# A decoder trunk on one core: residual and gate tiles turned onto feature partitions by VectorE blocks and small DMAs in place of TensorE transposes

## The chip, the cores and the metric

The kernel runs on one core of a Trainium2 chip. The metric is the device time of one execution in microseconds (us), all inputs in DRAM at the start and the output in DRAM at the end. The five engines are called PE (TensorE; its weight loads are listed apart as PEld), DVE (VectorE), ACT (ScalarE), POOL (GpSimd) and SP (SyncE, which here only issues DMAs). All tensors are fp32; for the matmuls a value is split in two parts, "hi" and "lo", in the type fp32r.

## The reference, cut to what matters

One layer on 256 tokens with 2048 features; x and every residual sum have the shape (256, 2048).

```python
h = x
h = h + hybrid_mixer(rmsnorm(h, norm_mix), w_in, ...)          # ends in a product with w_out (4096 x 2048)
h = h + memory_cross_attention(rmsnorm(h, norm_xa), mem_n, w_q, w_k, w_v, w_o)   # 4 heads of 128
h = h + swiglu(rmsnorm(h, norm_ffn), w_gate, w_up, w_down)     # 2048 -> 5632 -> 2048
return rmsnorm(h, norm_final)

def rmsnorm(x, g):
    return x * rsqrt(mean(x * x, axis=-1, keepdims=True) + 1e-5) * g
def swiglu(h, w_gate, w_up, w_down):
    return (silu(h @ w_gate) * (h @ w_up)) @ w_down
```

A product that contracts over features needs its left operand with the features on the 128 partitions. The residual tiles after `w_out` and `w_o`, and the gate tiles after `w_gate` and `w_up`, come out of PSUM with the tokens on the partitions. They have to be turned between the two products. That turning is what the change is about.

## The kernel before

**Weights.** All weights come as one stream of tiles of 128 x 1024 fp32 (512 KB), in the order in which they are used (`stream_plan`, 537 tiles). A tile is known by its kind and numbers: `("wo", n, c)` for w_out, `("q", t, c)`, `("o", n, c)`, `("g", n, c)` and `("u", n, c)` for gate and up, `("d", n, c)` for down. `load_to(k)` (lines 144 to 153) issues the loads of the stream up to tile k - 1 on SP; line 151 is the DMA, and six buffers `r` (pool "raw", bufs=6) receive them. `split_to(k)` (lines 155 to 169) makes the hi part on ACT (line 165) and the lo part on DVE (line 166), four buffers `h` and `l` each. So the load of tile i waits until the split of tile i - 6 has read its buffer, and that split waits until PE is through with tile i - 10.

**Units and steps.** The program is written as a row of units, two weight tiles each in the stages spoken of here. Of one unit:

```python
load_to(last + AHEAD - 1)        # AHEAD = 6
split_to(last + 1)
for i, (ks, fn) in enumerate(parts):
    fn()                         # the matmuls of one part
    if i == 0:
        step()                   # each waiting post-processing generator goes on to its next yield
        split_to(last + 3)
load_to(last + AHEAD)
```

What has to be done with a unit's result (evacuate, square, turn) is a generator such as `wo_post`, `o_post` or `u_post`; it is appended after the unit, and a piece of it, up to the next `yield`, is written into the program in the `step()` of each later unit. **PE and SP run strictly in the order in which the program is written** (line 112). The order on ACT, DVE and POOL is chosen when the kernel is built by a planner that works with its own assumed costs; at run time each engine follows its list in order.

**A DMA's place.** SP executes its list in order, so a DMA that waits holds all loads behind it. The DMAs of a queue engine take turns on eight completion semaphores: a DMA waits until the one eight before it has landed.

**Token-major products.** `tok_mm` (lines 789 to 798) does twelve matmuls for a weight tile: two feature blocks, two token blocks `tb`, and for each the three products of hi and lo parts (lines 796, 797, 798). The q projection contracts in the other orientation, through `mm_hi` and `mm_lo` (lines 294 and 300).

**Turning.** `add_to_res(n, ...)` (lines 808 to 814) adds the PSUM result of a column group n (512 features) to the two residual tiles (line 812) and squares them on ACT (line 814). `to_features(n, gain, dst)` (lines 816 to 827) turns the two 128 x 512 tiles with eight PE transposes of 128 x 128 into PSUM tiles `m` (line 823), and `hilo_scaled` scales and splits each of four features blocks out of PSUM: ACT line 179, DVE line 180. In `wo_post` and `o_post` it comes one step after `add_to_res`. `u_post(n)` multiplies the gate (line 1008), and one step later turns it with eight transposes (line 1015) and splits it (ACT line 1018, DVE line 1019). There are 4 groups after w_out (`"nxa"` gains), 4 after w_o (`"nffn"` gains), and 11 gate groups.

**Who needs them.** The features 8 to 15 of the first residual (groups 2 and 3) are used by `q_rest(0)`, the first q part with c = 1, which follows the four parts with c = 0. The features 2c and 2c + 1 of the second residual are used by gate tile `("g", 0, c)`, so group n is first used in c = 2n. The gate features are used only in the down stage, after all gate and up tiles.

**The order between w_o and gate.** This part is written out by hand (lines 963 to 988) and then goes on in units:

```python
ahead(("o", 1, 1), 2)     # loads up to ("g", 0, 0)
o_mm(0, 3)                # last matmuls of group 0; appends o_post(0)
step()                    # first piece of o_post(0)
o_mm(1, 3)                # last matmuls of group 1; appends o_post(1)
for n in (2, 3): unit(...)   # groups 2 and 3, two weight tiles each
```

Of the kernel before, what the change touches and what calls it, by code (L numbers as in the profile page):

```python
# [13 lines left out]
F32 = mybir.dt.float32  # L14
F32R = mybir.dt.float32r
AF = mybir.ActivationFunctionType
ALU = mybir.AluOpType
# [3 lines left out]
T = 256  # L21
# [47 lines left out]
def stream_plan():  # L69

    p = []
    p += [(("k0",), 512), (("v0",), 512)]
    for kt in range(1, KT):
        p.append((("kv", kt), 1024))
    p += [(("a", t, c), 1024) for c in range(2) for t in FIRST]
    for _, m, t, _ in mixer_order():
        p += [((m, t, c), 1024) for c in range(2)]
    for n in range(4):
        p += [(("wo", n, c), 1024) for c in range(KT)]
    p += [(("q", t, c), 1024) for c in range(2) for t in range(4)]  # L80
    p += [(("o", n, c), 1024) for n, c in [(0, 0), (1, 0), (0, 1), (1, 1), (2, 0), (2, 1), (3, 0), (3, 1)]]
    for n in range(FN):
        for m in "gu":
            p += [((m, n, c), 1024) for c in range(KT // 2)]
    for n in range(4):
        p += [(("d", n, c), 1024) for c in range(FT // 2)]
    return p


def trunk(tc, wst, vecs, xp, xtp, mp, wdt_in, nfin, outp):  # L90
    nc = tc.nc
    plan = stream_plan()
    index = {k: i for i, (k, _) in enumerate(plan)}
    offs, o = [], 0
# [5 lines left out]
    with ExitStack() as ctx:  # L100
        E = ctx.enter_context
# [4 lines left out]
        sp = E(tc.tile_pool(name="slots", bufs=65))  # L106
        tp = E(tc.tile_pool(name="tmp", bufs=8))
        gtp = E(tc.tile_pool(name="gate", bufs=4))
        accp = E(tc.tile_pool(name="acc", bufs=4, space=PSUM))
        mscp = E(tc.tile_pool(name="msc", bufs=4, space=PSUM))  # L110
        drp = E(tc.tile_pool(name="scr", bufs=1, space=DRAM))
# [61 lines left out]
        def v(name, i):  # L173
            return vec[:, VOFF[name] + i:VOFF[name] + i + 1]

        def hilo_scaled(src, gain):

            a = slot(dt=F32R)
            act(a[:, 0:T], src, AF.Identity, scale=gain)  # L179
            stt(a[:, T:], src, gain, a[:, 0:T].bitcast(F32), ALU.mult, ALU.subtract)  # L180
            return a
# [22 lines left out]
        def small(name):  # L204
            return cp.tile([128, 2], F32, tag=name, name=nm(name), bufs=4)
# [110 lines left out]
        ident = cp.tile([128, 128], F32, name="ident")  # L316
# [462 lines left out]
        res = [[None] * 4 for _ in range(2)]  # L779
# [28 lines left out]
        def add_to_res(n, accs, sums):  # L808

            for tb in range(2):  # L810
                h = res[tb][n]
                tt(h, accs[tb], h, ALU.add)
                j = gtp.tile([128, 512], F32, tag="g", name=nm("j"))
                act(j, h, AF.Square, accum_out=sums[:, tb, n:n + 1])

        def to_features(n, gain, dst):

            for i in range(2):
                ps = msc()
                for f in range(2):  # L820
                    for tb in range(2):
                        o = (2 * i + f) * 128
                        nc.tensor.transpose(ps[:, f * T + tb * 128:f * T + tb * 128 + 128],  # L823
                                            res[tb][n][:, o:o + 128], ident)
                for f in range(2):
                    t = 4 * n + 2 * i + f
                    dst[t] = hilo_scaled(ps[:, f * T:f * T + T], v(gain, t))

        def token_scale(name, sums, factor=None):

            e = small("rv")
            with tc.high_priority():
                nc.vector.tensor_reduce(e, sums, axis=mybir.AxisListType.X, op=ALU.add)
            r = inv_rms(e, D)
            out = cp.tile([128, 2], F32, name=name)
            ts(out, r, 1.0 if factor is None else factor, None, ALU.mult)
            return out


        h1g = {}  # L840
# [3 lines left out]
        def wo_post(n, accs):  # L844
            add_to_res(n, accs, h1s)
            if n == 0:
                act(small("rv"), half, AF.Exp)
            if n == 3:
                xa["sc"] = token_scale("xsc", h1s, XSCALE)
            yield  # L850
            to_features(n, "nxa", h1g)

        for n in range(4):
            accs = [acc(), acc()]
# [57 lines left out]
        h2g = {}  # L912
# [2 lines left out]

        def o_post(n, accs):
            add_to_res(n, accs, h2s)
            if n == 3:
                ff["r"] = token_scale("fscale", h2s)
            yield  # L920
            to_features(n, "nffn", h2g)

        oacc = {}

# [66 lines left out]
        gate = {}  # L991
# [11 lines left out]
        def u_post(n, accs):  # L1003
            while n not in gate:
                yield
            for tb in range(2):
                s = gate[n][tb]
                stt(s, accs[tb], ff["r"][:, tb:tb + 1], s, ALU.mult, ALU.mult)
            yield
            for i in range(2):  # L1010
                ps = msc()
                for f in range(2):
                    for tb in range(2):
                        o = (2 * i + f) * 128
                        nc.tensor.transpose(ps[:, f * T + tb * 128:f * T + tb * 128 + 128],  # L1015
                                            gate[n][tb][:, o:o + 128], ident)
# [19 lines left out]
        gain = []  # L1036
# [94 lines left out]
    return np.ascontiguousarray(a.T.reshape(8, 2, 128, T).transpose(0, 2, 1, 3).reshape(8, 128, 512))  # L1131


def _cols(a):

    import numpy as np
    a = np.asarray(a)
    n = a.shape[0] // 128
    return a.reshape(n, 128, -1).transpose(1, 0, 2).reshape(128, -1)


def _weights(i):
    import numpy as np
    w_in = np.asarray(i["w_in"])[0]
    blk = {}

# [6 lines left out]
    blk["q"] = tiles(np.asarray(i["w_q"])[0], 8)  # L1153
    rows = {m: np.asarray(i[k])[0].reshape(-1, 2, 128, i[k].shape[-1] // 512, 512).transpose(3, 0, 2, 1, 4)
            for m, k in (("wo", "w_out"), ("o", "w_o"), ("g", "w_gate"), ("u", "w_up"), ("d", "w_down"))}
    wk, wv = np.asarray(i["w_k"])[0], np.asarray(i["w_v"])[0]
    plan = stream_plan()
    out = np.empty(sum(128 * w for _, w in plan), np.float32)
    p = 0
    for key, w in plan:  # L1160
        m = key[0]
        if m == "k0":
            c = wk[0:128]
        elif m == "v0":
            c = wv[0:128]
        elif m == "kv":
            s = slice(key[1] * 128, key[1] * 128 + 128)
            c = np.concatenate([wk[s], wv[s]], axis=1)
        elif m in rows:
            c = rows[m][key[1], key[2]]  # L1170
        else:
            c = blk[m][key[1]][:, 8 * key[2]:8 * key[2] + w // 128]
        out[p:p + 128 * w] = c.reshape(-1)
        p += 128 * w
    return out


def _vectors(i):
    import numpy as np
    g = {k: np.asarray(a) for k, a in i.items() if a.ndim <= 3}  # L1180
    part = {
        "nmix": _cols(g["norm_mix"][0]), "nmem": _cols(g["mem_norm"]), "nxa": _cols(g["norm_xa"][0]),
        "nffn": _cols(g["norm_ffn"][0]), "nssd": _cols(g["ssd_norm"][0]),
        "nsc": _cols(g["sc_norm"][0]), "cw": _cols(g["ssd_conv_w"][0].T), "cb": _cols(g["ssd_conv_b"][0]),
        "sw": _cols(g["sc_conv_w"][0].T), "dsk": _cols(np.repeat(g["d_skip"][0], 64)),
        "dtb": np.broadcast_to(g["dt_bias"][0], (128, H)), "alog": np.broadcast_to(g["a_log"][0], (128, H)),
    }
    return np.ascontiguousarray(np.concatenate([part[n] for n, _ in _W], axis=1))
# [33 lines left out]
```

## Time and profile before

| | |
|---|---|
| median of 3 runs | 1558.4 us (1558.07 to 1558.67) |
| the profiled execution's own time | 1558.37 us |
| its span, first to last instruction | 1556.7 us |
| mean granted PE clock | 0.998 |
| busy: PE, PEld, DVE, ACT, POOL | 99%, 83%, 59%, 52%, 3% |
| DMA | 300.66 MB, mean 193 GB/s |

The span is 1.67 us shorter than the profiled execution's time, and that execution is within 0.03 us of the median. The stages after the mixer's input projections are: w_out from 582.5 us on, the q projection from 760.1 us, attention and w_o to 816.9 us, gate and up from there, and then down. Matmuls are pipelined: a matmul of 512 columns shows as 0.39 us in the profile, but one starts every 0.23 us. Times between starts are therefore what the prediction counts with.

### The profile page before, as it was taken

To read this page: it belongs to the slowest core of one execution; us is meant where nothing else is said; L and a number is where in the kernel's file an instruction comes from. 1 tells how busy PE (TensorE), PEld (TensorE's weight loads), DVE (VectorE), ACT (ScalarE), POOL (GpSimd) and SP (SyncE) were. 2 spreads that over 40 slices of the span, in tenths; PEclk is the share of its full clock that TensorE was granted. 3 is DMA by queue.
4 is the path that set the end of the run, shared out by engine and by line. 5 is a ranking of instruction groups with operands and counts; after the bars stand their busy time and mean duration, and the time that the engine had idled before them with its cause. 6 is when DMAs were issued, how large, how long until landed. Compare 5 with 4: busy or idle time off the path is not lost.

```text
span 1556.7 us, 20300 instructions
## 1 busy us (share of the span) xinstructions
PE 1541.9 (99%) x7716; PEld 1294.6 (83%) x7716; DVE 916.8 (59%) x1214; ACT 805.3 (52%) x1157; POOL 46.6 (3%) x65
## 2 busy tenths in 40 slices
PE   9999999999999999999999999999999999999997
PEld 7888888888888888888888888888888888888886
DVE  5976886776776674555575555545455555455453
ACT  6685775774765454444465444444444444344342
POOL 0011300100000000000000000000000000000000
PEclk9999999999999999999999999999999999999999
DMA  9665655655655556665545555555555556656662
GB/s 346 248 199 192 217 173 181 209 183 173 220 170 183 173 186 199 203 202 202 191 134 183 189 184 193 189 197 189 189 189 188 183 194 209 201 191 195 194 191 95
DMA packets 92962, 300.66 MB, mean 193 GB/s; under 512 B 9888, under 2 KB 18496, under 8 KB 92864
## 3 DMA queue, kind: packets, MB, share of 16 engines
q1 hardware_dynamic: 83664, 291.98, 56.4%
q10 hardware_dynamic: 9200, 7.39, 1.6%
q8 instruction: 60, 0.98, 0.2%
q14 instruction: 38, 0.31, 0.1%
HBM read 297.19 MB, written 2.15 MB: 192 GB/s over the span
## 4 chain that ended last, share of the span: by engine, by line
PE 96%; DMA 2%; ACT 1%; DVE 0%; issue 0%; SPq 0%; POOLq 0%; POOL 0%; DVEq 0%; ACTq 0%
PE a L294 21%; PE a L796 20%; PE a L798 20%; PE a L797 20%; PE a L300 11%; DMA s<-in_m_dram 1%; PE m L1015 1%; PE m L674 1%; DMA r<-in_w_dram 0%; PE m L823 0%; PE m L200 0%; ACT h L165 0%; DMA s<-in_x_dram 0%; PE m L242 0%; PE a L516 0%
## 5 line engine op out<-in xcount | busy, mean ns | idle before, releaser
L166 DVE TENSOR_TENSOR l<-r,h 128x1024 fp32r<-128x1024 f32 (+2 forms) x555 | 657.2, 1193 | 537.0 <-ACT h L165 464.4
L165 ACT CAST h<-r 128x1024 fp32r<-128x1024 f32 (+2 forms) x555 | 564.5, 1022 | 629.2 <-PE a L798 475.3
L796 PE MATMUL a<-h,s 128*128 128x512 f32 x1344 | 525.7, 391 | 0.0
L798 PE MATMUL a<-h,s 128*128 128x512 f32 x1344 | 523.2, 389 | 0.0
L797 PE MATMUL a<-l,s 128*128 128x512 f32 x1344 | 523.0, 389 | 0.0
L294 PE MATMUL a<-s,h 128*128 128x512 f32 x1472 | 370.4, 397 | 0.3 <-ACT h L165 0.3
L294 PEld LDWEIGHTS a<-s,h 128*128 128x128 f32 x1472 | 265.5, 188 | 52.9 <-issue 2.6
L798 PEld LDWEIGHTS a<-h,s 128*128 128x128 f32 x1344 | 252.3, 188 | 52.8
L797 PEld LDWEIGHTS a<-l,s 128*128 128x128 f32 x1344 | 252.4, 188 | 51.7
L796 PEld LDWEIGHTS a<-h,s 128*128 128x128 f32 x1344 | 252.3, 188 | 51.3
L300 PEld LDWEIGHTS a<-s,l 128*128 128x128 f32 x1472 | 188.9, 191 | 7.8
L300 PE MATMUL a<-s,l 128*128 128x256 f32 x1472 | 191.4, 282 | 0.0
L192 ACT COPY t<-a 128x256 f32<-128x256 f32 x96 | 35.1, 369 | 36.9 <-PE a L300 36.6
L615 DVE SCALAR_TENSOR_TENSOR t<-t,vec,t 128x255 f32<-128x255 f32 (+2 forms) x72 | 34.9, 485 | 6.3 <-ACT t L612 5.5
L235 POOL TENSOR_TENSOR rr<-rv,half 128x2 f32<-128x2 f32 x24 | 16.6, 692 | 646.4 <-DVE rv L234 629.4
L193 DVE TENSOR_TENSOR t<-a,t 128x256 f32<-128x256 f32 x76 | 31.9, 419 | 5.0 <-ACT t L192 3.8
L516 PE MATMUL a<-s,h 128*128 128x512 f32 x64 | 25.1, 421 | 1.5 <-DVE s L180 1.4
L1074 POOL TENSOR_TENSOR fr<-fr,half 128x1 f32<-128x1 f32 x2 | 1.9, 942 | 726.7 <-DVE fr L1073 726.7
L1000 ACT ACTIVATE g<-a,fscale 128x512 f32<-128x512 f32 x22 | 15.0, 690 | 9.9 <-PE a L798 9.9
L517 PE MATMUL a<-s,l 128*128 128x256 f32 x64 | 18.6, 290 | 0.6 <-DVE l L166 0.6
L179 ACT ACTIVATE s<-m,vec 128x256 fp32r<-128x256 f32 x32 | 14.2, 470 | 9.4 <-DVE s L180 9.2
L616 ACT ACT_TABLE_LOAD x12 | 15.4, 1283 | 6.1 <-DVE t L615 3.1
(163 smaller groups left out, 680.8 us busy)
## 6 DMA issues: line engine op xcount, KB each, us to landing
r<-in_w_dram SPq DMA_DIRECT2D x535, 512.0 KB, 3.3
s<-acsT ACTq DMA_DIRECT2D x24, 256.0 KB, 6.1
s<-in_xt_dram SPq DMA_DIRECT2D x16, 256.0 KB, 5.7
s<-in_x_dram SPq DMA_DIRECT2D x8, 256.0 KB, 7.2
s<-in_m_dram SPq DMA_DIRECT2D x7, 256.0 KB, 7.2
s<-in_nfin_dram SPq DMA_DIRECT2D x4, 256.0 KB, 3.8
out_dram<-s SPq DMA_DIRECT2D x4, 256.0 KB, 3.1
out_dram<-s ACTq DMA_DIRECT2D x4, 256.0 KB, 3.7
```

Source lines behind the costliest of these rows:

```text
L165: nc.scalar.copy(h[:, c], r[:, c])
L166: tt(l[:, c], r[:, c], h[:, c].bitcast(F32), ALU.subtract)
L192: nc.scalar.copy(t, ps[:, T:])
L193: tt(dst, ps[:, 0:T], t, ALU.add)
L294: mm(ps, h[:, k * 128:k * 128 + 128], acts[k0 + k], start=start and k == 0, stop=False)
L300: mm(ps[:, 0:T], l[:, k * 128:k * 128 + 128], acts[k0 + k][:, 0:T], start=False, stop=stop and k == n - 1)
L516: mm(kacc[t], h[:, t * 128:t * 128 + 128], a, start=s, stop=False)
L517: mm(kacc[t][:, 0:T], l[:, t * 128:t * 128 + 128], a[:, 0:T], start=False, stop=e)
L615: stt(a[:, d:], u[:, 0:T - d], v("cw", 4 * ct + k), a[:, d:], ALU.mult, ALU.add)
L796: mm(ps[tb], ah, h[:, w], start=start and i == ks[0], stop=False)
L797: mm(ps[tb], ah, l[:, w], start=False, stop=False)
L798: mm(ps[tb], al, h[:, w], start=False, stop=stop and i == ks[-1])
```

## The change

A tile pair is turned in two moves. `turn_blocks` makes two DVE instructions, each of which transposes every 32 x 32 block of a 128 x 512 tile in place of its block (features of a block on 32 partitions, the tokens along the free dimension), into a 128 x 1024 tile `b`. `spread` then moves blocks between partition groups with 16 DMAs on SP, 32 KB each: 32 partitions, two runs of 128 fp32 for each. It returns a view of the receiving tile `f`, whose features are in an order that differs from the natural one inside each group of 512; the rows of w_q, w_gate, w_up and w_down and the gains are put into that order on the host (`_turned`). ACT and DVE then make hi and lo parts out of SBUF instead of PSUM.

The places change too. In `wo_post` the turning stays a step after `add_to_res` for groups 0 to 2 and comes right after it for group 3; in `o_post` it comes right after `add_to_res` for all groups, ahead of `token_scale`. In `u_post` the DVE blocks come right after the multiplication, the DMAs a step later and the split another step later.

```diff
+        bp = E(tc.tile_pool(name="blocks", bufs=2))
+        fp = E(tc.tile_pool(name="feat", bufs=2))
...
+        def turn_blocks(src):
+            t = bp.tile([128, 1024], F32, tag="b", name=nm("b"))
+            for tb in range(2):
+                nc.vector.transpose(t[:, tb * 512:tb * 512 + 512], src[tb])
+            return t
+
+        def spread(t):
+            d = fp.tile([128, 1024], F32, tag="f", name=nm("f"))
+            tv = t.rearrange("p (t k) -> p t k", t=2)
+            dv = d.rearrange("p (t a c) -> p t a c", t=2, a=4)
+            for a in range(4):
+                for b in range(4):
+                    nc.sync.dma_start(dv[32 * b:32 * b + 32, :, a, :],
+                                      tv[32 * a:32 * a + 32, :, 128 * b:128 * b + 128])
+            return d.rearrange("p (x f j) -> p f x j", x=8, f=4)
+
         def to_features(n, gain, dst):
-            for i in range(2):
-                ps = msc()
-                for f in range(2):
-                    for tb in range(2):
-                        o = (2 * i + f) * 128
-                        nc.tensor.transpose(ps[:, f * T + tb * 128:f * T + tb * 128 + 128],
-                                            res[tb][n][:, o:o + 128], ident)
-                for f in range(2):
-                    t = 4 * n + 2 * i + f
-                    dst[t] = hilo_scaled(ps[:, f * T:f * T + T], v(gain, t))
+            d = spread(turn_blocks([res[tb][n] for tb in range(2)]))
+            for f in range(4):
+                g = v(gain, 4 * n + f)
+                a = slot(dt=F32R)
+                hi, lo = [a[:, i * T:i * T + T].rearrange("p (x j) -> p x j", x=8) for i in range(2)]
+                act(hi, d[:, f], AF.Identity, scale=g)
+                stt(lo, d[:, f], g, hi.bitcast(F32), ALU.mult, ALU.subtract)
+                dst[4 * n + f] = a
...
 wo_post
+            if n < 3:
+                yield
+            to_features(n, "nxa", h1g)
             if n == 3:
                 xa["sc"] = token_scale("xsc", h1s, XSCALE)
-            yield
-            to_features(n, "nxa", h1g)
...
 o_post
             add_to_res(n, accs, h2s)
+            to_features(n, "nffn", h2g)
             if n == 3:
                 ff["r"] = token_scale("fscale", h2s)
-            yield
-            to_features(n, "nffn", h2g)
+            return
+            yield
...
 u_post
+            t = turn_blocks(gate[n])
+            yield
+            d = spread(t)
             yield
             for i in range(2):
-                ps = msc()
...
                 hi, lo = slot(dt=F32R), slot(dt=F32R)
-                nc.scalar.copy(hi, ps)
-                tt(lo, ps, hi.bitcast(F32), ALU.subtract)
+                hv, lv = [a.rearrange("p (f x j) -> p f x j", f=2, x=8) for a in (hi, lo)]
+                nc.scalar.copy(hv, d[:, 2 * i:2 * i + 2])
+                tt(lv, d[:, 2 * i:2 * i + 2], hv.bitcast(F32), ALU.subtract)
                 gs[2 * n + i] = hi, lo
...
-    nc = bacc.Bacc("TRN2", target_bir_lowering=False, num_devices=1)
+    nc = bacc.Bacc("TRN2", target_bir_lowering=False, num_devices=1, dynamic_dma_scratch_size=1024)
```

The smaller scratch makes room in SBUF for the four new tiles of 4 KB per partition.

More of the change, by code (lines that the diff above doesn't have):

```diff
@@ L1008, in u_post @@
                 stt(s, accs[tb], ff["r"][:, tb:tb + 1], s, ALU.mult, ALU.mult)
+            t = turn_blocks(gate[n])
+            yield
+            d = spread(t)
             yield
             for i in range(2):
-                ps = msc()
[L1012 to L1016, printed above, removed]
                 hi, lo = slot(dt=F32R), slot(dt=F32R)
-                nc.scalar.copy(hi, ps)
-                tt(lo, ps, hi.bitcast(F32), ALU.subtract)
+                hv, lv = [a.rearrange("p (f x j) -> p f x j", f=2, x=8) for a in (hi, lo)]
+                nc.scalar.copy(hv, d[:, 2 * i:2 * i + 2])
+                tt(lv, d[:, 2 * i:2 * i + 2], hv.bitcast(F32), ALU.subtract)
                 gs[2 * n + i] = hi, lo
@@ L1131, in _pairs, with _turned @@
     return np.ascontiguousarray(a.T.reshape(8, 2, 128, T).transpose(0, 2, 1, 3).reshape(8, 128, 512))
+def _turned(a):
+    n, rest = a.shape[0] // 512, a.shape[1:]
+    return a.reshape((n, 4, 4, 32) + rest).swapaxes(1, 2).reshape((n * 512,) + rest)
 def _cols(a):
@@ L1152, in _weights @@
     blk["b"] = tiles(w_in[:, 5152:], 8)
-    blk["q"] = tiles(np.asarray(i["w_q"])[0], 8)
-    rows = {m: np.asarray(i[k])[0].reshape(-1, 2, 128, i[k].shape[-1] // 512, 512).transpose(3, 0, 2, 1, 4)
+    blk["q"] = tiles(_turned(np.asarray(i["w_q"])[0]), 8)
+    rows = {m: (_turned(np.asarray(i[k])[0]) if m in "gud" else np.asarray(i[k])[0]).reshape(-1, 2, 128, i[k].shape[-1] // 512, 512).transpose(3, 0, 2, 1, 4)
             for m, k in (("wo", "w_out"), ("o", "w_o"), ("g", "w_gate"), ("u", "w_up"), ("d", "w_down"))}
@@ L1181, in _vectors @@
     part = {
-        "nmix": _cols(g["norm_mix"][0]), "nmem": _cols(g["mem_norm"]), "nxa": _cols(g["norm_xa"][0]),
-        "nffn": _cols(g["norm_ffn"][0]), "nssd": _cols(g["ssd_norm"][0]),
+        "nmix": _cols(g["norm_mix"][0]), "nmem": _cols(g["mem_norm"]), "nxa": _cols(_turned(g["norm_xa"][0])),
+        "nffn": _cols(_turned(g["norm_ffn"][0])), "nssd": _cols(g["ssd_norm"][0]),
         "nsc": _cols(g["sc_norm"][0]), "cw": _cols(g["ssd_conv_w"][0].T), "cb": _cols(g["ssd_conv_b"][0]),
```

## The prediction

> **What bounds the kernel now.** I read the page first (busy shares and the chain that ended last), then the chain in order of time, then the waits of SP and ACT, then the timelines around the two places where turned tiles are needed soon.
>
> ```profile
> span 1556.7 us, 20300 instructions
> PE 1541.9 (99%) x7716; PEld 1294.6 (83%) x7716; DVE 916.8 (59%) x1214; ACT 805.3 (52%) x1157; POOL 46.6 (3%) x65
> PE 96%; DMA 2%; ACT 1%; DVE 0%; issue 0%; SPq 0%; POOLq 0%; POOL 0%; DVEq 0%; ACTq 0%
> ```
>
> PE is the bound: it makes 96% of the chain, so what PE no longer does is gained in full, unless PE then waits. The chain in order of time prices the turning, a group of eight in each of two stages:
>
> ```profile
> 768.65 0.87 PE m L823 x8
> 870.61 0.87 PE m L1015 x8
> ```
>
> ```profile
> SPq L151 <- DVE l L166: 1192.8, 469, 8.4
> ACT h L165 <- PE a L798: 469.6, 290, 2.4
> ```
>
> The waits show why PE never starves. SP, which will issue the new DMAs, stands idle most of the time until a split frees a weight buffer, and ACT waits for PE to free an `h`. Loads run up to ten tiles ahead of PE. That lead is what hides DMA work on SP, and it is finite.
>
> **What goes.** 19 groups of eight transposes (4 after w_out, 4 after w_o, 11 gate) x 0.87 = 16.5 us off PE. Nothing else leaves the chain: the splits stay, with SBUF in place of PSUM as source, which I cost at nothing since ACT and DVE have a third of their time free.
>
> **What comes on DVE: 38 block transposes of 128 x 512.** The trace has none.
>
> ```profile
> L812 DVE TENSOR_TENSOR s<-a,s 128x512 f32<-128x512 f32 x16 | 10.5, 685 | 1.5 <-PE a L798 1.4
> L1084 DVE TENSOR_SCALAR s<-s,fr 128x512 f32<-128x512 f32 x6 | 2.6, 480 | 0.1
> L179 ACT ACTIVATE s<-m,vec 128x256 fp32r<-128x256 f32 x32 | 14.2, 470 | 9.4 <-DVE s L180 9.2
> L180 DVE SCALAR_TENSOR_TENSOR s<-m,vec,s 128x256 fp32r<-128x256 f32 x32 | 14.6, 478 | 3.3 <-ACT s L179 3.3
> ```
>
> Bounds for one are 0.48 us (L1084) and the 0.75 us of L1008 below, which also are 512 elements per partition. I take 0.685 (L812, nearest in the middle): 26 us more on an engine with 640 us idle. Twice that would cost 1.4 us at each of the two places below.
>
> **What comes on SP: 19 x 16 = 304 DMAs of 32 KB.** Their issue time is the number that decides. The first two rows are the first and the last group of seven issues in a row on SP at the start (the last holds two), the next two a load and another DMA right behind it, the last two the first and the last of six in a row on ACT's queue.
>
> ```profile
> 1.22 0.42 SPq L332 DMA_DIRECT2D s<-in_m_dram  x1
> 4.06 0.91 SPq L151 DMA_DIRECT2D r<-in_w_dram  x2
> 712.82 0.33 SPq L151 DMA_DIRECT2D r<-in_w_dram  x1
> 713.20 0.42 SPq L783 DMA_DIRECT2D s<-in_xt_dram  x1
> 80.65 0.40 ACTq L576 DMA_DIRECT2D s<-acsT  x1
> 83.30 0.56 ACTq L576 DMA_DIRECT2D s<-acsT  x1
> ```
>
> ```profile
> q10 hardware_dynamic: 9200, 7.39, 1.6%
> r<-in_w_dram SPq DMA_DIRECT2D x535, 512.0 KB, 3.3
> acsT<-s ACTq DMA_DIRECT2D x1, 48.0 KB, 2.2
> vec<-in_v_dram SPq DMA_DIRECT2D x1, 8.0 KB, 1.8
> ```
>
> From one start to the next it takes (4.06 - 1.22) / 6 = 0.47 us on SP with one run per partition, (83.30 - 80.65) / 5 = 0.53 us on ACT with several runs per partition, and 0.38 us at the least (713.20 - 712.82). The new ones are on SP with two runs per partition; I take 0.50, between the first two. Low end 0.38, high end 0.61 (the 0.56 of the slowest row and a gap of 0.05). A spread of 16 thus keeps SP 8.0 us. Data is no matter: q10's packets (800 B) took 1.6% x 16 x 1556.7 / 9200 = 0.043 us, and each DMA has 64 on 16 engines. After its issue the last DMA lands 1.8 to 2.2 us later; I take 1.9. Eight in flight at 0.50 us make 4 us, longer than a landing, so the eight semaphores do not hold the row up.
>
> One rule speaks against taking issue time as the term. "Issuing engines are not separate DMA queues" in "DMA: Bandwidth & Descriptors" of the Trainium skill says that the time a sequencer needs to start a DMA is usually small beside the DMA itself. By it the waits worked out below vanish and the span falls by the whole 16.5 us; by the rows one issue (0.42) is over twice the 4 x 0.043 us that its packets take on an engine, and I go by the rows.
>
> **Gate groups (11 of the 19): hidden.**
>
> ```profile
> 861.99 1.41 DVE L1008 SCALAR_TENSOR_TENSOR g<-a,fscale,g 128x512 f32<-128x512 f32 x2
> 859.39 3.05 SPq L151 DMA_DIRECT2D r<-in_w_dram  x2
> 876.99 1.05 ACT L165 CAST h<-r 128x1024 fp32r<-128x1024 f32 x1 [1.67 <-PE a L798]
> ```
>
> The multiplication ends at 863.4, the blocks at 864.8, the spread at 872.8. The second load of the SP row (about 862.1) is the first one behind it in SP's list: it lands at 872.8 + 3.3 = 876.1, and its split began at 876.99. So even the split is not late, and SP catches up, with 0.47 us per load against 2.72 us per tile on PE. The features are used only in the down stage. The three early w_out groups go the same way. Without that cover a spread would cost up to its 8 us.
>
> **w_o to gate: not hidden.** Here four spreads follow one another within four units, and in SP's list they stand between the loads of the first gate tiles: spread 0, load g(0,1), spread 1, g(0,2), g(0,3), spread 2, g(0,4), g(0,5), spread 3, g(0,6).
>
> ```profile
> 802.43 1.37 DVE L812 TENSOR_TENSOR s<-a,s 128x512 f32<-128x512 f32 x2 [1.25 <-PE a L798]
> 804.38 1.28 DVE L812 TENSOR_TENSOR s<-a,s 128x512 f32<-128x512 f32 x2
> 788.14 0.33 SPq L151 DMA_DIRECT2D r<-in_w_dram  x1
> 810.35 0.33 SPq L151 DMA_DIRECT2D r<-in_w_dram  x1
> 826.04 1.03 PE L823 MATMUL m<-ident,s 128*128 128x128 f32 x8
> 826.28 1.05 ACT L165 CAST h<-r 128x1024 fp32r<-128x1024 f32 x1 [1.00 <-ACT s L179]
> 827.36 1.22 DVE L166 TENSOR_TENSOR l<-r,h 128x1024 fp32r<-128x1024 f32 x1 [0.80 <-ACT h L165]
> 835.09 0.39 PE L796 MATMUL a<-h,s 128*128 128x512 f32 x1
> ```
>
> Before, SP had issued g(0,1) at 788.14 and g(0,6) at 810.35, and PE began g(0,6) at 835.09: 25 us of lead. After, group 0 is added by 803.8 and turned by 805.2, where spread 0 begins. Four spreads (32.0) and five loads (5 x 0.47) later, at 839.5, SP issues g(0,6); it lands at 842.8, and with cast 1.05 and lo part 1.22, less the 0.23 of the first matmul, which needs no lo, PE begins it at 844.9. Without waiting PE would begin it at 835.09 - 4 x 0.87 = 831.6. So PE waits 13.3 us, in three pieces of about 6, 3.5 and 3.5 at g(0,2), g(0,4) and g(0,6). The turned features come earlier than those loads: spread 3 lands at 840.9, its first split is done at 841.9. After g(0,6) SP issues load after load and PE isn't held again. By the ends of the issue time this term is 64 x 0.38: 5.6 us, or 64 x 0.61: 20.3 us.
>
> **w_out to q: a little.**
>
> ```profile
> 759.65 1.37 DVE L812 TENSOR_TENSOR s<-a,s 128x512 f32<-128x512 f32 x2
> 768.49 1.04 PE L823 MATMUL m<-ident,s 128*128 128x128 f32 x8
> 772.15 2.00 PE L294 MATMUL a<-s,h 128*128 128x512 f32 x8
> 778.42 2.20 PE L294 MATMUL a<-s,h 128*128 128x512 f32 x8
> ```
>
> Group 3 is added by 761.0 and turned by 762.4; the last DMA goes out 15 x 0.50 later, lands at 771.8, and the four splits (0.47 + 4 x 0.48) end at 774.2. PE needs the last at 772.15 - 0.87 + 7 x 0.23 = 772.9: 1.3 us of waiting, 0 to 3 by the ends. The first load behind this spread, q(2,1), goes out at 770.4, lands at 773.7 and is split by 776.0; PE came to it at 778.42, now 0.87 earlier, and the later ones have more room.
>
> **Sum.** -16.5 + 13.3 + 1.3 = -1.9 us: 1558.37 - 1.9 = 1556.5 us against the profiled execution, whose time is that of the median within 0.03. The ends give 1558.37 - 10.9 = 1547.5 and 1558.37 + 6.8 = 1565.2. The sign hangs on hundredths of a us: at 0.52 us per DMA nothing is gained or lost.
>
> **Rivals.**
>
> *Issues are cheaper.* At 0.38 us each, 1547.5 us. For it: the row at 713.20. Against: two in a row are not sixteen, and all longer rows are slower. Chance 0.25, which includes 0.03 that the waits vanish (1541.9).
>
> *Slower: the groups turn one after the other through DVE.* DVE follows its list. If the splits of group 1, which wait for spread 1, stand there ahead of the addition of group 2, then spread 2 cannot begin at 822.6 but only when spread 1 has landed (823.1), four splits (2.4), an addition (1.4) and a turn (1.4) are done: 828.3. Likewise spread 3: 842.9 to 850.9, and PE begins g(0,6) at 856.2, 11.3 us later than above: 1567.8 us. If it happens at group 3 alone, 1562.1. It decides the sign as soon as one group is held by 2 us.
>
> ```profile
> 811.02 1.28 DVE L812 TENSOR_TENSOR s<-a,s 128x512 f32<-128x512 f32 x2
> 815.79 0.48 DVE L180 SCALAR_TENSOR_TENSOR s<-m,vec,s 128x256 fp32r<-128x256 f32 x1
> ```
>
> Against it: before, the addition of group 2 (811.02) stood ahead of the splits of group 1 (815.79). For it: those splits are now written a step earlier, and the list is fixed before the run, without the time that SP takes. Chance 0.27.
>
> *The clock falls in the new pauses.*
>
> ```profile
> 785.00:805.00 20.00, 19.05 (x94) 15.85 (x93) 12.25 (x29) 11.87 (x32) 0.00 (x0) 1.00 0.32 106
> 1550.00:1556.00 6.00, 0.00 (x0) 0.00 (x0) 1.25 (x3) 0.72 (x1) 0.00 (x0) 0.51 0.83 290
> ```
>
> With 0.95 us of pauses the granted clock stayed at 1.00; in the last 6 us, without matmuls, it was 0.51. After the pauses at g(0,2) and g(0,4) slow matmuls cost nothing, since the next load is what PE waits for. After the last, 3.5 us at 0.51 would cost 1.7 us: 1558.2. Chance 0.06. "Part 1: The HAM clock gate" in "TensorE: Matmul & The Clock Gate" of the Trainium skill has the clock halve after an idle window of about 3.4 us, for as long again; by it the sum would be that 1.7 us worse.
>
> **How the numbers follow.** Forecast 0.42 (own range 1553 to 1562), cheaper issues 0.25, DVE in series 0.27, clock 0.06. The range 1547 to 1568 reaches the three rivals. A time within 0.2% (3.1 us) cannot be told from no change here. Faster: 0.25 and 0.12 of the forecast's lower side, 0.37. Same: 0.27. Slower: 0.27, 0.06 of the forecast's upper side and 0.03 of the clock, 0.36.
>
> **What the changed profile would show.** PE's transposes of `m` from `s` and `g` gone; 38 DVE transposes near 0.69 us; SP issues in rows of 16 at 0.50 us; between 805 and 850 PE idle for about 13 us in three pieces that end with a split whose load had just landed; no idle PE in the gate stage. Wrong would be: idle PE in every gate group, waits that end with the features' splits in place of loads, or an issue time outside 0.45 to 0.55.

## The result, and the profile after

The changed kernel takes 1576.39 us (median of 4 runs, 1575.57 to 1577.6) against 1558.38 us before (4 runs): a ratio of 1.0117, interval 1.0105 to 1.013. It is 18 us slower, where 1556.5 was forecast and 1568 was the upper end. The profiled execution took 1577.6 us with a span of 1575.6, 18.9 more than before. All traces below are set against each other by their own spans.

The page of the changed kernel, beginning with the lines that answer to those shown of before (span, busy shares, chain by engine), then the chain by line, the waits with the longest idle PE, and the DMA issues (KB each, us to landing):

```profile
span 1575.6 us, 20491 instructions
PE 1538.8 (98%) x7564; PEld 1285.1 (82%) x7564; DVE 938.4 (60%) x1252; ACT 806.8 (51%) x1157; POOL 45.5 (3%) x65
PE 85%; SPq 5%; DMA 3%; ACT 2%; DVE 2%; issue 1%; ACTq 0%; POOLq 0%; POOL 0%; DVEq 0%
PE a L296 20%; PE a L799 17%; PE a L800 17%; PE a L798 17%; PE a L302 10%; SPq L833 5%; DMA r<-in_w_dram 3%; ACT h L167 1%; DVE l L168 1%; PE m L676 1%; DVE s L814 0%; PE m L202 0%; DVE b L822 0%; PE m L244 0%; PE a L518 0%
L798 PE MATMUL a<-h,s 128*128 128x512 f32 x1344 | 527.8, 393 | 14.9 <-ACT h L167 13.0
r<-in_w_dram SPq DMA_DIRECT2D x535, 512.0 KB, 4.3
f<-b SPq DMA_DIRECT2D x304, 32.0 KB, 1.9
```

PE fell from 96% to 85% of the chain, and SP's own time, which was 0% of it, is now 5%: all of it is L833, the line that issues the small DMAs. SP had been idle most of the time and still became what PE waits for, because it is asked for 41 us of issues within one stretch. L798, the first matmul of a weight tile, now waits 13.0 us for `h` of L167, the hi part of a weight tile.

Where the 19 us lie, by the start of the first matmul of each stage in the two traces (after minus before, growth within the stretch):

| stretch | starts, before and after | predicted | measured |
|---|---|---|---|
| to the first w_out matmul | 582.59, 582.83 | 0 | +0.25 |
| w_out, to its last matmul | 759.91, 759.99 | -2.6 | -0.17 |
| q and attention, to the first w_o matmul | 788.70, 794.32 | +0.4 | +5.54 |
| w_o and gate group 0, to u(0,0) | 840.53, 869.49 | +9.8 | +23.34 |
| the rest of gate and up, and down, to the last matmul | 1546.61, 1565.58 | -9.6 | -9.99 |
| sum | | -1.9 | +18.97 |

The stretch that decides is w_o to gate. SP's timeline there:

```profile
810.68 10.19 SPq L833 DMA_DIRECT2D f<-b  x16
820.97 0.53 SPq L153 DMA_DIRECT2D r<-in_w_dram  x1
821.60 10.18 SPq L833 DMA_DIRECT2D f<-b  x16
831.88 1.01 SPq L153 DMA_DIRECT2D r<-in_w_dram  x2
832.99 10.95 SPq L833 DMA_DIRECT2D f<-b  x16
843.98 1.06 SPq L153 DMA_DIRECT2D r<-in_w_dram  x2
845.45 10.18 SPq L833 DMA_DIRECT2D f<-b  x16
855.68 6.10 SPq L153 DMA_DIRECT2D r<-in_w_dram  x7
```

This is the list of the prediction, spread 0, g(0,1), spread 1, g(0,2) and g(0,3), and so on, back to back, with one gap of 0.4 us (ahead of 845.45). But a row of sixteen takes 10.2 us and not 8.0: one issue begins (820.97 - 810.68) / 16 = 0.64 us after the other. So g(0,6) goes out at 855.68, 45 us after the row began. PE's and ACT's timelines at the other end of that load, with PE's earlier pauses:

```profile
775.93 2.07 PE L296 MATMUL a<-s,h 128*128 128x512 f32 x4 [3.47 <-DVE s L845]
822.90 0.50 PE L798 MATMUL a<-h,s 128*128 128x512 f32 x1 [1.95 <-ACT s L844]
836.52 0.79 PE L798 MATMUL a<-h,s 128*128 128x512 f32 x1 [6.72 <-ACT h L167]
848.54 0.51 PE L798 MATMUL a<-h,s 128*128 128x512 f32 x1 [2.69 <-ACT h L167]
859.12 1.04 ACT L167 CAST h<-r 128x1024 fp32r<-128x1024 f32 x1 [0.26 <-DMA r<-in_w_dram]
860.22 0.75 PE L798 MATMUL a<-h,s 128*128 128x512 f32 x1 [3.31 <-ACT h L167]
861.48 0.79 PE L799 MATMUL a<-l,s 128*128 128x512 f32 x1 [0.51 <-DVE l L168]
```

In brackets stands how long the engine was idle and who ended it. The first two pauses end with features (group 3 of w_out at q, group 0 of w_o at g(0,0)), the next three with a weight tile whose load had just landed: g(0,2), g(0,4), g(0,6), the three places that were predicted. The pause at g(0,0) was not forecast. PE reaches g(0,6) at 860.22. From 835.09, plus the 5.62 us by which PE came late to w_o, less 4 x 0.87 for the transposes, it would have been there at 837.2: it lost 23.0 us. A second loss stands in the first number of the rows, a duration: the matmuls behind the pauses at g(0,2) and g(0,6) take 0.75 to 0.79 us where 0.39 is usual (the one at 822.90, at full clock, 0.50). Busy time and granted clock by window (the clock is third from the right):

```profile
774.00:782.00 8.00, 6.07 (x19) 5.12 (x20) 5.42 (x11) 5.39 (x11) 0.00 (x0) 0.57 0.97 371
835.00:840.00 5.00, 3.02 (x6) 2.11 (x7) 3.51 (x5) 2.09 (x2) 0.00 (x0) 0.50 0.49 147
860.00:865.00 5.00, 4.27 (x9) 3.06 (x10) 3.23 (x3) 2.83 (x4) 0.00 (x0) 0.53 0.96 383
```

### The profile page after: what moved, and what is told of

Read it like the earlier page. It is cut to its first block, busy times and chain, and to the rows that moved or that the text cites. A ratio compares the mean times of both kernels' runs of the same rounds, so it can differ in the third digit from the quotient of the medians.

```text
span 1575.6 us, 20491 instructions
## 1 busy us (share of the span) xinstructions
PE 1538.8 (98%) x7564; PEld 1285.1 (82%) x7564; DVE 938.4 (60%) x1252; ACT 806.8 (51%) x1157; POOL 45.5 (3%) x65
## 4 chain that ended last, share of the span: by engine, by line
PE 85%; SPq 5%; DMA 3%; ACT 2%; DVE 2%; issue 1%; ACTq 0%; POOLq 0%; POOL 0%; DVEq 0%
PE a L296 20%; PE a L799 17%; PE a L800 17%; PE a L798 17%; PE a L302 10%; SPq L833 5%; DMA r<-in_w_dram 3%; ACT h L167 1%; DVE l L168 1%; PE m L676 1%; DVE s L814 0%; PE m L202 0%; DVE b L822 0%; PE m L244 0%; PE a L518 0%
## 5 line engine op out<-in xcount | busy, mean ns | idle before, releaser
L167 ACT CAST h<-r 128x1024 fp32r<-128x1024 f32 (+2 forms) x555 | 564.2, 1022 | 591.2 <-PE a L800 389.9
L798 PE MATMUL a<-h,s 128*128 128x512 f32 x1344 | 527.8, 393 | 14.9 <-ACT h L167 13.0
L798 PEld LDWEIGHTS a<-h,s 128*128 128x128 f32 x1344 | 254.0, 189 | 69.7 <-ACT h L167 14.7
L302 PE MATMUL a<-s,l 128*128 128x256 f32 x1472 | 192.2, 283 | 0.0
L844 ACT ACTIVATE s<-f,vec 128x256 fp32r<-128x256 f32 x32 | 13.7, 497 | 42.3 <-DMA f<-b 42.3
L845 DVE SCALAR_TENSOR_TENSOR s<-f,vec,s 128x256 fp32r<-128x256 f32 x32 | 13.4, 480 | 28.5 <-ACT s L844 28.5
L1037 ACT CAST s<-f 128x512 fp32r<-128x512 f32 x22 | 12.6, 619 | 25.0 <-DMA f<-b 25.0
L1038 DVE TENSOR_TENSOR s<-f,s 128x512 fp32r<-128x512 f32 x22 | 14.2, 688 | 18.4 <-ACT s L1037 18.4
```

Source lines behind the costliest of these rows:

```text
L167: nc.scalar.copy(h[:, c], r[:, c])
L302: mm(ps[:, 0:T], l[:, k * 128:k * 128 + 128], acts[k0 + k][:, 0:T], start=False, stop=stop and k == n - 1)
L798: mm(ps[tb], ah, h[:, w], start=start and i == ks[0], stop=False)
```

## The experiments

The theory after the first look: 16 issues of 0.64 us in a row on SP hold back loads (w_o to gate) or features (q), and the slow clock after each pause adds to it; the gate stage by itself gains all that was forecast. Rivals: the route itself is slow (DVE, landing, features), the order around w_o is at fault and not the issues, or 0.64 us is a matter of size or partitions that other shapes would avoid.

**Only the gate groups by DMAs.** `wo_post` and `o_post` go back to eight PE transposes:

```diff
-            to_features(n, "nffn", h2g)      # o_post, and likewise wo_post
+            yield
+            to_features_pe(n, "nffn", h2g)   # eight transposes, as before
```

> The 11 gate groups turn by DVE blocks and DMAs, both residual stages by TensorE as before. In the changed kernel every gate group from g(2) on ran 0.91 us faster than before and the two residual places lost 28.9 us. Theory (SP's 16 issues of 0.64 us hold the loads and features only where the turned tiles are needed soon): 11 x 0.91 = 10.0 us faster than before, 1548.4 us, no PE idle time in the gate stage. Rival (the DMAs disturb all loads, or the planner's new lists cost in all stages): 1555 or more.

Measured 1548.76 us, ratio 0.9938 (0.9923 to 0.9953). In the trace one gate group follows the other after 43.52 us in place of 44.43, and PE has no pause there. So the eleven gate groups give their 10.0 us in full within their stage (the medians differ by 9.2), and the loss belongs to the eight residual groups.

**w_out and gate by DMAs, w_o by TensorE.** The same edit in `o_post` alone.

> Only the groups after w_o go back to TensorE; those after w_out and the gate stay with blocks and DMAs. Theory: the place between w_o and gate cost 23.3 us net (+5.64 at o(2,0), +28.96 at u(0,0)), so 1576.4 - 23.3 = 1553.1 us, with a pause of 3.5 us at q_rest(0) left. Rival (one cost moves into the other, for instance loads late from the q stage on): 1560 or more.

Measured 1553.4 us, 0.9968 (0.9956 to 0.9981). Between this kernel and the changed one lie 23 us: what the four w_o groups cost. Between it and the one before lie 4.6 us: what the four w_out groups cost on balance, after the 3.5 us of transposes that they save. The pause at q is still in PE's row of waits (us in total, times, longest):

```profile
PE a L296 <- DVE s L845: 4.3, 1, 4.3
```

**The same bytes in 4 DMAs instead of 16.** Left out is the exchange between partition groups: each group of 32 partitions is copied to itself.

```diff
-                for b in range(4):
-                    nc.sync.dma_start(dv[32 * b:32 * b + 32, :, a, :],
-                                      tv[32 * a:32 * a + 32, :, 128 * b:128 * b + 128])
+                nc.sync.dma_start(d[32 * a:32 * a + 32, :], t[32 * a:32 * a + 32, :])
```

> The same bytes in 4 DMAs of 128 KB for each group of 16 of 32 KB; left out is the exchange between partition groups, so the values are not the reference's. Theory (number of issues): 4 x 0.64 = 2.6 us on SP for each spread, 15.4 us in place of 41 between w_o and g(0,6); all waits go and 1542 to 1544 us remain. Rival (bytes, landing times, or DVE and ACT lists that wait for the spread in series): 1565 to 1577 us.

Measured 1543.38 us, 0.9905 (0.9891 to 0.992). SP's timeline at the same place:

```profile
801.20 2.42 SPq L832 DMA_DIRECT2D f<-b  x4
803.72 0.53 SPq L153 DMA_DIRECT2D r<-in_w_dram  x1
804.35 2.43 SPq L832 DMA_DIRECT2D f<-b  x4
...
818.63 2.42 SPq L832 DMA_DIRECT2D f<-b  x4
821.10 8.69 SPq L153 DMA_DIRECT2D r<-in_w_dram  x8
```

Four times the bytes in an issue leave its price where it was, (803.72 - 801.20) / 4 = 0.63 us. DVE blocks, splits and order are those of the changed kernel, and 33 us are gone. So the number of issues is the cost, not the bytes, the turning on DVE, or the place of the steps. The shape of a DMA changed with the number (one run of 4 KB per partition in place of two of 512 B); the version through DRAM below, which does the whole exchange in five issues, is 26.5 us faster than the changed kernel and bears the reading out.

**What sets 0.64.** To the kernel with only the gate groups by DMAs, each gate group 0 to 9 gets eight more DMAs of one shape, which nobody uses (two of the 65 buffers `s` give the room for their tile).

```diff
+                if n == 0:      # 32 partitions, two runs each, SBUF to SBUF
+                    nc.sync.dma_start(d2(x[q:q + 32, :])[:, :, ...], d2(t[0:32, :])[:, :, 0:128])
...
+                elif n == 2:    # 32 partitions, one run each, from one piece of DRAM
+                    nc.sync.dma_start(x[q:q + 32, c:c + 256], w1)
```

> For the issue time alone: in the kernel with only the gate groups turned by DMAs, gate groups 0 to 9 each issue 8 more DMAs on SP behind their 16, of one shape per group, into a tile that nobody reads. Before the change loads from DRAM over 128 partitions started every 0.47 us at the closest. If the number of runs per partition makes the 0.64 us, one run per partition should go at about 0.47; if the small number of partitions does, 128 partitions from SBUF should; if a source in SBUF does, all shapes from DRAM should stay near 0.47 and all shapes from SBUF near 0.64; if it is the short descriptor list, 16 partitions should be quicker. The time should stay at 1549 to 1551, since gate groups have more than 10 us of room.

The issues on SP by line: durations in ns (shortest, median, longest), starts of the first and the last of eight. In order: SBUF to SBUF on 32 partitions with two runs each, with one run each, on 128 and on 16 partitions; then one piece of DRAM to SBUF, on 32 partitions with one run each, the same piece with two runs each, and on 128 partitions with one run each.

```profile
L846 SPq DMA_DIRECT2D x<-b x8: 594/595/596, 875.2 to 879.7; - x8
L848 SPq DMA_DIRECT2D x<-b x8: 586/588/592, 922.3 to 926.8; - x8
L854 SPq DMA_DIRECT2D x<-b x8: 594/599/606, 1059.7 to 1064.2; - x8
L860 SPq DMA_DIRECT2D x<-b x8: 587/588/592, 1199.3 to 1203.7; - x8
L850 SPq DMA_DIRECT2D x<-in_w_dram x8: 414/419/582, 969.0 to 972.4; - x8
L852 SPq DMA_DIRECT2D x<-in_w_dram x8: 592/592/595, 1013.0 to 1017.5; - x8
L856 SPq DMA_DIRECT2D x<-in_w_dram x8: 430/430/593, 1106.9 to 1110.4; - x8
```

From SBUF to SBUF an issue takes 0.59 to 0.60 us (4.5 / 7 = 0.64 from start to start) whatever the partitions (16, 32, 128), and with one run as with two. From one piece of DRAM it takes 0.42 to 0.43 (0.47 from start to start) with one run per partition, and 0.59 with two: L850 and L852 read the same 32 KB of DRAM and differ only in the runs in the tile. The time, 1579.18 us in one run, missed the expectation by far and told something else: 24 issues (15.4 us) between the loads of a gate group are more than its lead hides. By the starts of the gate groups, 43.52 us apart without the extra DMAs, the groups behind the dear shapes lost 2.1 to 4.6 us each, and those behind the three cheap ones (16 x 0.64 + 8 x 0.47 = 14.0 us of issues) still 1.0 to 1.7. So the cover of the gate stage is above 10.2 and below 14.0 us of issues.

**Every second DMA on ACT's queue.**

```diff
-                    nc.sync.dma_start(
+                    (nc.scalar if b % 2 else nc.sync).dma_start(
```

> Every second of the 16 DMAs is issued on ACT's queue. Theory (issue time on SP's list): 5.1 us per spread on SP, about 2 us of waiting between w_o and gate, 1544 to 1548 us unless ACT's 8 x 0.6 us per spread delay the splits. Rival (both queues share what makes the descriptors, so the total rate stays at one per 0.64 us): 1570 to 1577 us.

Measured 1565.8 us, 1.0053 (1.0038 to 1.0068), between the two. The timeline of both queues in the first w_o spread, then ACT's own timeline there and its waits from 560 us on:

```profile
804.74 2.53 SPq L833 DMA_DIRECT2D f<-b  x4
805.04 2.59 ACTq L833 DMA_DIRECT2D f<-b  x4
802.18 5.45 ACTq L833 DMA_DIRECT2D f<-b  x8
807.68 0.63 ACT L816 ACTIVATE j<-s 128x512 f32<-128x512 f32 x1 [5.06 <-DMA f<-b]
ACT h L167 <- DMA f<-b: 95.9, 15, 8.0
```

Four in 2.53 us and four in 2.59 at the same time: each queue keeps its 0.64 us, so the rate doubles. But the issues stand in ACT's list, and what is behind them waits: ACT's eight take 5.45 us, of which ACT stands idle for 5.06. Casts of weight tiles were held for 95.9 us in 15 waits, where the changed kernel has 3.3 in 2; issues on ACT run for 79 us of these 95.9, and only the rest of it is a wait for something else. At w_out, with time to spare, the 2.7 us of groups 0 to 2 were kept and PE came to w_o 2.9 us ahead of before. From there to u(0,0) it lost 18.0 us, where the changed kernel lost 23.3, and its three long pauses end with casts of weight tiles.

**Matmuls that keep the clock up in the pauses.** 12 useless matmuls at q, 24 each behind g(0,1), g(0,3) and g(0,5).

```diff
+            if m == "g" and n == 0 and c in (1, 3, 5):
...
+                for _ in range(24):
+                    mm(wp, h2g[0][:, 0:128], h[:, 0:512], start=True, stop=True)
```

> The changed kernel, with matmuls of no use put into the four longest pauses (12 at q_rest(0), 24 each behind g(0,1), g(0,3), g(0,5), 2.7 and 5.5 us), so that PE never idles for long. Theory (a pause of 3 us or more lets the granted clock fall to 0.5 for 3.4 or 6.8 us, and what of that runs behind a pause that isn't followed by another one is lost: 2.9 us at q, 3.8 us from g(0,6) on): 6 to 7 us faster than the changed kernel, 1569.5 to 1570.5 us. Rival (the low clock only fills time that PE would wait anyway): 1576 us or more.

Measured 1573.91 us (1572.72 to 1575.09), 1.0101 (1.0084 to 1.0118). The window behind g(0,6):

```profile
860.00:865.00 5.00, 5.00 (x23) 4.12 (x22) 3.36 (x4) 3.32 (x4) 0.00 (x0) 1.00 1.02 410
```

The clock stays at 1.00, and 3.0 of the 3.8 us lost between g(0,6) and u(0,0) come back. At q only 0.9 us do: PE waits for the features all the same, and at full clock it soon runs into another pause:

```profile
781.37 1.10 PE L901 MATMUL m<-s,t 128*128 128x256 f32 x4 [1.14 <-DVE t L195]
```

Together that is 3.9 us by the trace and 2.5 by the medians, not the 6 that the theory expected: the clock's cost is confirmed in kind, its size only in part.

**Loads ahead of the first w_o spread.** If the order is at fault, g(0,1) to g(0,3) issued ahead of it should help.

```diff
+        load_to(index[("g", 0, 4)])
         step()
```

> The changed kernel with the loads of g(0,1), g(0,2), g(0,3) issued ahead of the first spread after w_o instead of between the spreads. Theory (SP's whole list of 64 issues is the chain; the next thing late is the features themselves): the pauses at g(0,1) and g(0,2) end with features' splits, g(0,6) still begins after all four spreads, 1 to 2 us earlier at most: 1574 to 1576 us. Rival (only the place of the loads in the list matters, the features come early enough): the pauses up to g(0,3) go for good, 1560 to 1566 us.

Measured 1573.42 us, 1.0097 (1.0082 to 1.0112). The pause at g(0,2) became one for features:

```profile
830.91 0.79 PE L798 MATMUL a<-h,s 128*128 128x512 f32 x1 [4.46 <-ACT s L844]
```

Three of 18 us come back. A list that is too long stays too long in another order.

**Paced.** w_out groups 0 to 2 by DMAs, four in each of four steps, split a step later; w_out group 3 and w_o by TensorE; gate by DMAs.

```diff
+            for a in range(4):
+                for b in range(4):
+                    nc.sync.dma_start(dv[32 * b:32 * b + 32, :, a, :], ...)
+                yield
```

> Gate groups by DMAs as in the change; w_out groups 0 to 2 too, but with 4 of the 16 DMAs in each of four steps, and their splits a step later; w_out group 3 and all of w_o by TensorE. Theory (rows of 16 hold loads for 10 us, rows of 4 for 2.6 us, less than the room that loads have): the 2.6 us of PE time of these three groups are gained in full, 1548.8 - 2.6 = 1546.2 us, no pauses in the w_out stage. Rival (the DMAs' number matters there however they are placed, or the late splits hold ACT's list): 1548.5 us or more.

Measured 1545.33 us (1545.14 to 1545.84), 0.9916 (0.9901 to 0.993): 13 us less than before and 31 less than the changed kernel. PE's only wait from 560 us on is the old one in attention:

```profile
PE m L955 <- ACT s L950: 0.9, 1, 0.9
```

The w_out groups, which by rows of 16 gave 0.17 us in all, now keep 2.7 us.

**Through DRAM, 5 issues for a group.** One DMA writes `b` to DRAM, four fetch it with the exchange. In one version the fetch stands a step behind the write (at once for w_out group 3 and w_o group 0), in the other right behind it everywhere.

```diff
+            nc.sync.dma_start(sc, t)                      # 512 KB
...
+            sv = sc.rearrange("(a c) (t b k) -> b c t a k", a=4, t=2, b=4)
+            for b in range(4):
+                nc.sync.dma_start(dv[32 * b:32 * b + 32], sv[b])
```

> All 19 groups are turned by the same DVE blocks, but the exchange goes through DRAM: one DMA of 512 KB writes b, four of 128 KB fetch it, one for each group of 32 partitions (runs of 512 B). 5 issues in place of 16 at 0.64 us: 3.2 us of SP for a group in place of 10.2. The fetch comes a step after the write, so that SP goes on with loads while the write lands, but at once for w_out group 3 and w_o group 0, where SP is held for the landing (3.1 us by the row of the output's DMAs, 256 KB). Theory (what costs is the number of issues on SP between loads): w_o to gate 6.3 + 3 x 3.2 + 5 x 0.63 = 19 us of list, less than the 25 us of lead, so no wait at g(0,6); the row at q ends at about 768.6 and costs 0 to 1 us; all 19 x 0.87 to 0.91 kept: 1541 to 1544 us. Rival (small pieces or the longer way through DRAM cost the time, not the issues: 1 MB more of DMA work for each group, later features): pauses at q and at g(0,0) to g(0,4) that end with the features' splits, 1550 us or more.

> As the one before, but the fetch stands right behind the write for all groups, where the spread stood, so SP is held for each landing of the write. Theory: per group 5 x 0.64 + about 3 us of holding = 6.3 us; w_o to gate 4 x 6.3 + 5 x 0.63 = 28.4 us of list against 25 of lead, and g(0,6) about 7 us late: 1548 to 1552 us. Rival (waits in SP's list cost nothing, since DMAs are asynchronous): same time as the version with the fetch a step later.

Measured 1549.84 us (0.9946, 0.9934 to 0.9959) and 1558.58 us (1.0002, 0.9993 to 1.0011). The second missed its range of 1548 to 1552, the first its range too (below). The first version's DMA issues and waits of PE (page, and waits from 560 us on):

```profile
f<-scr SPq DMA_DIRECT2D x76, 128.0 KB, 5.2
PE a L798 <- ACT s L847: 4.3, 3, 2.0
PE a L296 <- DVE s L848: 1.5, 1, 1.5
```

No load is late any more, so this half of the theory holds; but the fetches land 5.2 us after issue (the small ones 1.9) and the features come late: half of the rival holds too, and 1541 to 1544 was too low. The second version holds SP between write and fetch:

```profile
819.30 0.38 SPq L830 DMA_DIRECT2D scr<-b  x1
825.82 3.68 SPq L834 DMA_DIRECT2D f<-scr  x4
```

6.5 us from the write to the fetch where 3.1 were assumed; the write goes out right behind two loads of 512 KB (with no load in flight, at 804.01, the fetch followed after 2.7). The run takes 8.7 us more than the first version, so a DMA that waits in SP's list is not free. The row of the write also limits what the probe says of SBUF: with SBUF as source but DRAM as target, its issue takes 0.38 us, and 0.33 where SP had been idle. A row of such writes was not run.

## Why the prediction was wrong, point by point

**The step that failed is the issue time.** 0.50 us per DMA was taken, with 0.61 as the end; it is 0.64. Behind it is a choice of rows. The row of seven at 1.22 (0.47) has DRAM as source and one run per partition, and the probe shows that this is the cheap kind. The row of six on ACT (0.53) was nearer but read as an upper neighbour. Two runs per partition do raise the price when the source is DRAM (0.42 against 0.59), as the prediction supposed, but from SBUF to SBUF one run is as dear, and the trace of before has no DMA from SBUF to SBUF. It has a dearer row on SP, which the prediction did not show:

```profile
5.59 1.26 SPq L337 DMA_DIRECT2D s<-in_xt_dram  x2
```

Two in 1.26 us are 0.63 each. What makes them dear is open: a DMA of the same tensor later (L785 at 687.38 in the changed kernel) takes 0.38 us, and the next issue follows it after 0.48. The low end, 0.38, came from a lone pair. In a probe row the first issue, right behind dear ones, takes 0.58 and the next ones 0.42 (longest and median of L850), so a single issue can show its neighbour's price, and a row of one kind is needed to see its own. With 0.64 in place of 0.50 the prediction's own formula gives 805.2 + 64 x 0.64 + 5 x 0.47 + 5.4 = 853.9 for g(0,6), which is 22.3 us of waiting (it measured 23.0, predicted 13.3), and at q 3.4 (it measured 3.47, predicted 1.3). The mechanism, the three places and what ends the pauses there were right; the term was mis-sized, and since 64 issues hang on it, 0.14 us became 9.0 of the 9.7 us that are missing there. The pause of 1.95 us at g(0,0), which ended with features, was one of the things that the prediction had named as signs of being wrong, and an issue time outside 0.45 to 0.55 another. PE's way to g(0,6) hangs on SP's list all the same, so that pause adds nothing to the sum. The prediction had said that the sign turns at 0.52. With 0.64 alone its sum is 1558.4 - 16.5 + 22.3 + 3.4 = 1567.6 us, inside its range: the step above gives about half of the miss, and the two terms below the rest.

The Trainium skill's rule ("DMA: Bandwidth & Descriptors", "Issuing engines are not separate DMA queues", that issue time is usually small beside the DMA) would have made it 1541.9. Here it fails: the issue of a 32 KB DMA takes 0.59 us of the 1.9 to its landing, and the experiment that cut their number to a quarter gave 33 us. The other half of that passage of the Trainium skill, that a second engine saves only the sequencer's time, agrees with the two queues at 0.64 us side by side; here that time is most of the cost.

**The clock was a rival with 0.06 and 1.7 us, and came on top of the forecast.** The windows above show 0.50 to 0.57 behind the pauses; PE took 6.1 us from g(0,6) to g(0,7) in place of 2.7, 3.8 us to u(0,0) in all (0.5 of it is the wait at 861.48 for the lo part), and lost about 2.9 at q. The slow stretches in the trace last 3.41, 6.83 and 10.24 us, and one followed a pause of 2.69 us. The Trainium skill's window of about 3.4 us ("TensorE: Matmul & The Clock Gate", "Part 1: The HAM clock gate") agrees with these multiples. The prediction's 1.7 us, one slow stretch of 3.5 us after the last pause alone, did not hold. Taking the slow clock away has shown 2.5 to 3.9 us of these 6.7; the rest is read from the trace alone.

**w_out groups 0 to 2 were costed at nothing, and were not hidden.** The stage kept 0.17 of 2.6 us. ACT's timeline there, where a tile comes late behind a row of 16 that also holds the residual's own loads (L785):

```profile
692.16 1.05 ACT L167 CAST h<-r 128x1024 fp32r<-128x1024 f32 x1 [3.41 <-DMA r<-in_w_dram]
```

"The three early w_out groups go the same way" was carried over from the gate stage without looking at what else stands in SP's list there. Paced DMAs show that the cover exists for four issues at a time; that the residual's loads are what makes a row of 16 too long was not tried by itself.

**The sum.** From -1.9 to +18.97: waits to the gate 9.7, at q 2.2, clock 6.7 (2.9 and 3.8), w_out groups 2.4, the start 0.25, less 0.4 that the gate stage gave beyond its term. That makes 20.9.

**What was right.** Eight transposes for 0.87 us: 0.91 in the gate stage. The landing at 1.9 (in the page above). The DVE block at 0.685, which is luck in part, since that figure was only the middle one of three rows of other instructions:

```profile
L822 DVE STREAM_TRANSPOSE b<-g 128x512 f32<-128x512 f32 x22 | 14.2, 685 | 0.0
```

The gate groups hidden: no idle PE in that stage. The rival of DVE in series did not occur: SP's rows stand back to back, and no spread waited for more than the 0.4 us at 845.45. Its 1567.8 us are nearer to the result than the forecast, by another mechanism.

## What to carry to other kernels

Count the DMA issues that a queue gets between two loads that are needed soon, and price one by a row of the same source, target and runs: here 0.47 us from DRAM with one run per partition, 0.64 us with two and from SBUF to SBUF, there from 8 KB to 128 KB. A cover is a length: ten us of issues vanished in a stage with a steady lead and cost 23 us where four such rows met a lead of 25 us, so spread them over steps, or leave the few urgent pieces on the busy engine. If the sign of a forecast hangs on hundredths of a us, give the range the dearest row of the trace as its end, and ask what a pause does to the clock.

## What the runs showed of the hardware that was not expected

- The issue price follows both ends of the DMA: 0.42 to 0.43 us from one piece of DRAM with one run per partition, 0.59 us with two runs, and 0.59 to 0.60 us from SBUF to SBUF, equal for 8 KB on 16 partitions and 128 KB on 32. Writes of 512 KB from SBUF to DRAM took 0.33 to 0.38 us.
- SP and ACT issue side by side without slowing each other: four in 2.53 and four in 2.59 us at once. But ACT's issues are time of ACT: 5.06 us idle for eight of them.
- After pauses of 2.7 to 6.7 us PE's granted clock was 0.5 for 3.41, 6.83 or 10.24 us; the starts of these stretches (774.97, 832.99, 850.06, 860.30) lie whole multiples of 3.41 us apart.
- The length of a pause does not decide by itself whether the clock falls. Through DRAM (first version), a pause of 2.00 us (813.54 to 815.54) was followed by 3.41 us at 0.5, from 815.91 on; with four DMAs per group, one of 2.43 us (817.30 to 819.73) was followed by none. On the grid of 3.41 us that the slow stretches of each trace set, the first lies whole in one window, and the second is cut into 0.91 and 1.52 us. In all twelve traces (before, changed kernel, ten experiments), between 500 and 1500 us, every window at full clock in which no matmul ran for 1.87 us or more was followed by a slow one, and none with less than 1.58 was. The stretches behind the two pauses (clock third from the right):

```profile
815.90:819.30 3.40, 3.40 (x10) 2.58 (x9) 2.82 (x7) 3.40 (x5) 0.67 (x1) 0.50 0.88 252
819.00:823.00 4.00, 3.27 (x14) 2.74 (x15) 4.00 (x7) 2.19 (x3) 0.00 (x0) 1.00 0.62 133
```

- A write to DRAM that follows two loads kept its reader waiting for 6.5 us, one with no load in flight (at 804.01) 2.7, and fetches of 128 KB among loads landed after 5.2 us (3.0 where the fetch stood right behind the write).
